# Two encoder layers on one Trainium2 core: the feed-forward's first norm applied as token factors behind the up projection

## The chip, the core and the metric

The kernel runs on one core of a Trainium2 chip. Its engines are TensorE (PE: matmuls; PEld: its weight loads), the vector engine (DVE), the scalar engine (ACT), GpSimd (POOL) and the engine that issues most loads (SP). Each works through its own list of instructions in order, and semaphores tie them together. SBUF has 128 partitions; matmul results land in PSUM, in banks of 128 x 512 float32. The metric is device time in microseconds (us) for one execution; 0.2% of it is 3 us.

## The reference, cut to what matters

Two layers act on x, 512 positions (tokens) of 1024 channels. Each has a token-mixing sub-layer and a feed-forward, and each of these has a norm before and a norm behind it. What the change touches is the end of the mixing sub-layer and the feed-forward:

```python
def rms_norm(x, g):
    y = xf * lax.rsqrt(jnp.mean(xf * xf, axis=-1, keepdims=True) + RMS_EPS)
    return y * g
...
    x = x + rms_norm(merged @ w_out[l], g_post_mix[l])
    h = rms_norm(x, g_pre_ffn[l])
    u = depthwise_conv_centred(h @ w_up[l], conv_w[l], conv_b[l])
    a, b = jnp.split(u, 2, axis=-1)
    f = jax.nn.gelu(a) * b
    x = x + rms_norm(f @ w_down[l], g_post_ffn[l])
```

`w_out` is 1024 x 1024, `w_up` 1024 x 5632, `w_down` 2816 x 1024. The convolution has width 3 and runs over positions, for each channel by itself. The factor rsqrt(...) is one number per token; the gain g is one number per channel.

## The kernel before, in words

**Layout.** Channels lie on partitions, tokens along the free axis. x is eight tiles of 128 channels x 512 tokens. A matrix of weights is cut into column tiles of 128 outputs; one tile of `w_up` or `w_out` is 128 x 8 x 128 (eight steps of 128 input channels, 512 KB).

**Split numbers.** Every operand of a large matmul is kept as two float32r numbers, a rounded high part and the rest. `split` (lines 220 to 222) makes them: a copy on ACT writes `hi`, a subtraction on DVE (or GpSimd) writes `lo`. One step of an output tile is three matmuls (`mm3`, line 246): high by high, high by low, low by high. A full tile has 8 steps of 512 columns (24 matmuls), a half tile 8 steps of 256.

**Weights.** `weights` (line 224) loads a tile into one of three buffers `wraw` and splits it, either into `whi` and `wlo` (two buffers each) or into buffers of another pool that are held longer (`m`, 32 buffers; `ka`, 12; `h`, 16).

**Order.** The program is written out by a Python generator in one order, and each engine executes its share of that order. `Woven` (line 46) keeps an estimate of TensorE's clock while matmuls are written. A job is a generator that yields a delay or a flag; `tick` runs the jobs that have come due between two steps of a tile, so their instructions land between the matmuls; `need` runs jobs until a flag is given. On TensorE this order is fixed by dependences; a matmul of a job stands where the job came due, and whatever is behind it waits with it.

**A norm.** `rstd_job` (line 323) sums squares over channels with matmuls against a column of 1/1024 (`mean`), takes the root on ACT and the reciprocal on DVE. That gives one factor per token, with tokens on partitions (`st`). To use it on tiles whose tokens lie on the free axis, it builds a diagonal matrix (two DVE multiplications of the identity, `h<-ident,st`) and multiplies it with a matrix of ones: the bank `pt` then has each token's factor in all 128 rows. The norms work on half the tokens (256) at a time; all 18 of the program go this way.

**The end of a mixing sub-layer** (`sublayer_end`, line 741, with `n_half` = 8). All eight tiles of `w_out` are done for half 0 (two at a time at first), then for half 1. ACT squares each result, DVE adds up the squares. When a half is complete, `end_job` (line 361) is spawned: norm, then per 128 channels a multiplication and the addition to x, and new squares in `acc2`; 9 us later `pre_norm_job` (line 347) makes the second norm from `acc2` and writes h = x * g * factor, split, for that half.

**The group.** Beside this stand six tiles of the up projection (0, 22, 1, 23, 2, 24; `run_group`, line 430), whose weights were split on GpSimd: half 0 of all six as soon as half 0 of h is there, then half 1. Two tiles go at a time. Their six banks are held until the convolution reads them.

**The loop** (line 860). For each of 22 pairs of up tiles j and j + 22: load and split weights, 24 matmuls into an `mm` bank (three banks), and `conv` (line 730): ACT writes y = bank * w1 + b, and two DVE operations of 511 columns add the neighbours, read from the bank. Gelu on ACT, the product and the split of the result on DVE. The weights of a tile are written directly before its matmuls. Then `sublayer_end` again, for `w_down` (three parts of weights per tile, 22 steps), with the last one or two tiles by halves, and in layer 0 the memory norm of layer 1 (`mem_norm_job`: squares on ACT, added up on GpSimd).

In the trace nearly all matmuls bear line 244 (`mm`), and nearly all ACT and DVE operations line 114, since helpers record them; the tile names tell them apart.

## Time and profile before

| | before |
|---|---|
| median of 3 runs (lowest, highest) | 1579.44 us (1579.17, 1579.61) |
| the profiled execution, its span | 1579.04 us, 1577.3 us |
| PE busy | 1529.7 us, 97% |
| PEld busy | 1316.4 us, 83% |
| DVE busy | 911.2 us, 58% |
| ACT busy | 727.4 us, 46% |
| GpSimd busy | 186.4 us, 12% |
| moved by DMA | 144.96 MB, 92 GB/s on average |
| mean granted clock of TensorE | 0.995 of full speed |

The span is the time from the first to the last instruction that the profile shows; the execution's own time is 1.7 us more. Busy time is the sum over an engine's instructions. 97% for PE means that about 48 us of the span hold no matmul; where they lie is not told by a share of the span, but by windows and by the column "idle before" of the timeline, which names the instruction that released the waiting one. The granted clock is the speed that the chip let TensorE have: 1.00 is 2.4 GHz, and the lower of its two levels is 1.2 GHz.

### The profile page before, as it was taken

The numbers are of one execution on the slowest core, as the hardware profiler recorded it, in microseconds if no ns is written. First come the engines' busy times: TensorE is split into PE (matmuls) and PEld (weight loads), VectorE is DVE, ScalarE is ACT, GpSimd is POOL, SyncE is SP. The second block draws the span as 40 slices with busy tenths as digits, with TensorE's granted clock in tenths as the row PEclk, the third lists the DMA queues.
The fourth block names the chain that finished last, engine by engine and source line by source line (L and its number), as shares of the span: only waits on it lengthen the run. The fifth ranks groups of instructions, "written<-read, shape, count | busy, mean of one in ns | idle before, by whom it ended". The sixth has DMA issues, their size and how long they took to land.

```text
span 1577.3 us, 21375 instructions
## 1 busy us (share of the span) xinstructions
PE 1529.7 (97%) x8246; PEld 1316.4 (83%) x8246; DVE 911.2 (58%) x1654; ACT 727.4 (46%) x1289; POOL 186.4 (12%) x244
## 2 busy tenths in 40 slices
PE   6999999999999999999989999999999999999997
PEld 5988888889898888878888888888898888888887
DVE  6686566344866666542386856743457666664233
ACT  5465575334544444532345646733454544444231
POOL 4340000110400000010062300001121000000000
PEclk9999999999999999999999999999999999999998
DMA  7222213224213222333331221132431232223331
GB/s 241 87 78 67 66 56 100 88 94 134 81 42 106 93 95 96 115 97 100 115 113 49 86 69 56 51 120 74 140 101 48 69 105 95 94 96 96 99 103 62
DMA packets 46614, 144.96 MB, mean 92 GB/s; under 512 B 5232, under 2 KB 11376, under 8 KB 46512
## 3 DMA queue, kind: packets, MB, share of 16 engines
q1 hardware_dynamic: 44656, 139.61, 27.7%
q10 hardware_dynamic: 1152, 2.10, 0.5%
q0 software_dynamic: 704, 1.88, 0.4%
q8 instruction: 65, 1.06, 0.3%
q14 instruction: 37, 0.30, 0.1%
HBM read 141.47 MB, written 2.10 MB: 91 GB/s over the span
## 4 chain that ended last, share of the span: by engine, by line
PE 88%; DVE 8%; ACT 2%; issue 1%; DMA 1%; SPq 0%; ACTq 0%
PE mm L244 73%; PE s L244 6%; PE o L244 3%; PE pt L244 2%; DVE h L114 2%; PE pt L255 2%; DVE y L114 2%; DVE x L114 1%; DVE m L114 1%; DVE wlo L114 1%; ACT whi L114 1%; DVE acc L114 1%; DVE ka L114 0%; ACT y L114 0%; DMA m<-in_memT_dram 0%
## 5 line engine op out<-in xcount | busy, mean ns | idle before, releaser
L244 PE MATMUL mm<-h,whi 128*128 128x512 f32 x2432 | 755.7, 392 | 0.0
L244 PEld LDWEIGHTS mm<-h,whi 128*128 128x128 f32 x2432 | 449.6, 188 | 88.7
L114 DVE TENSOR_TENSOR wlo<-wraw,whi 128x1024 fp32r<-128x1024 f32 (+1 forms) x203 | 246.9, 1218 | 394.9 <-ACT whi L114 394.8
L244 PE MATMUL mm<-h,wlo 128*128 128x512 f32 x1216 | 473.9, 390 | 0.0
L114 ACT CAST whi<-wraw 128x1024 fp32r<-128x1024 f32 (+1 forms) x203 | 210.3, 1038 | 296.5 <-PE mm L244 295.7
L244 PEld LDWEIGHTS mm<-h,wlo 128*128 128x128 f32 x1216 | 228.2, 188 | 48.5
L244 PE MATMUL mm<-m,whi 128*128 128x512 f32 (+1 forms) x672 | 178.2, 354 | 1.6 <-DVE m L114 0.8
L244 PEld LDWEIGHTS mm<-m,whi 128*128 128x128 f32 x672 | 119.6, 192 | 19.0 <-PE mm L244 1.3
L114 DVE SCALAR_TENSOR_TENSOR y<-mm,vec,y 128x511 f32<-128x511 f32 x160 | 118.9, 746 | 8.5 <-ACT y L114 5.9
L244 PE MATMUL mm<-m,wlo 128*128 128x512 f32 (+1 forms) x336 | 118.3, 352 | 0.7 <-DVE wlo L114 0.7
L114 ACT ACTIVATE y<-mm,vec 128x512 f32<-128x512 f32 (+1 forms) x163 | 113.6, 698 | 0.1
L244 PE MATMUL mm<-m,m 128*128 128x512 f32 (+1 forms) x432 | 88.6, 346 | 0.0
L222 POOL TENSOR_TENSOR m<-wraw,m 128x512 fp32r<-128x512 f32 x42 | 56.3, 1355 | 238.5 <-ACT m L114 234.2
L728 POOL TENSOR_TENSOR m<-m,y 128x512 f32<-128x512 f32 x28 | 36.1, 1289 | 405.7 <-DVE y L114 405.7
L244 PEld LDWEIGHTS mm<-m,m 128*128 128x128 f32 x432 | 67.6, 190 | 8.4
L244 PEld LDWEIGHTS mm<-m,wlo 128*128 128x128 f32 x336 | 64.4, 192 | 9.4 <-DVE wlo L114 1.1
L114 ACT ACTIVATE y<-y 128x512 f32<-128x512 f32 x44 | 27.8, 632 | 87.3 <-DVE y L114 87.3
L244 PE MATMUL mm<-h,m 128*128 128x256 f32 x456 | 63.6, 296 | 4.0 <-ACT h L114 1.6
L114 DVE TENSOR_TENSOR acc<-acc,sq 128x256 f32<-128x256 f32 (+1 forms) x86 | 44.6, 521 | 37.5 <-ACT sq L114 36.9
L114 ACT CAST m<-wraw 128x512 fp32r<-128x512 f32 (+1 forms) x98 | 56.1, 602 | 21.1 <-DMA wraw<-in_w_brb_dram 9.5
L244 PEld LDWEIGHTS mm<-h,m 128*128 128x128 f32 x456 | 59.2, 199 | 6.4 <-ACT h L114 2.8
L114 ACT CAST m<-pt 128x512 fp32r<-128x512 f32 (+1 forms) x72 | 38.2, 539 | 40.4 <-PE pt L255 32.0
(150 smaller groups left out, 1835.8 us busy)
## 6 DMA issues: line engine op xcount, KB each, us to landing
wraw<-in_w_in_dram SPq DMA_DIRECT2D x88, 512.0 KB, 3.3
wraw<-in_w_up_dram SPq DMA_DIRECT2D x88, 512.0 KB, 3.3
wraw<-in_w_down_dram SPq DMA_DIRECT2D x32, 512.0 KB, 3.5
wraw<-in_w_out_dram SPq DMA_DIRECT2D x16, 512.0 KB, 3.4
wraw<-in_w_down_dram SPq DMA_DIRECT2D x16, 384.0 KB, 3.1
wraw<-in_w_kv_dram SPq DMA_DIRECT2D x8, 512.0 KB, 3.6
wraw<-in_w_bra_dram SPq DMA_DIRECT2D x16, 192.0 KB, 2.3
x<-in_xT_dram SPq DMA_DIRECT2D x8, 256.0 KB, 7.2
```

Source lines behind the costliest of these rows:

```text
L114: return op(*args, **kw)
L222: last_lo[eng or V] = (eng or V).tensor_sub(lo, src, f32(hi)).ins
L244: wv.pe(nc.tensor.matmul(ps, a, b, start=first, stop=last), cost)
L255: wv.pe(nc.tensor.transpose(ps[:, 128 * i:128 * i + 128], s, ident), 0.11)
L728: (V if br == 2 and m >= 6 else G).tensor_add(acc[m], acc[m], gs)
```

## The change

**Broadcast.** `rstd_job` no longer builds a diagonal matrix. Per 128 tokens one matmul takes, as its weights, the column of factors read 128 times (stride 0) and multiplies it with the identity. The job yields 0.8 instead of 1.2 before it.

**End of the mixing sub-layer.** `n_half` goes from 8 to 4: `w_out` tiles 0 to 3 are full tiles, 4 to 7 half tiles. The group has four up tiles (0, 22, 1, 23) instead of six. Their weights are split on ACT and DVE, one tile after each of the four full tiles (`fill`). Four tiles go at a time in the group, with a flag per step of 128 channels.

**Factors.** In this place `factor_end_job` stands for `end_job` and `pre_norm_job`. It updates x as before, then splits x * g (without the factor of the second norm) as input of the up projection. The second norm's factors are worked out from the new x and copied to R, 128 x 512. Each up output is multiplied by R on DVE (`scaled`) on its way from the bank to SBUF, ahead of its convolution, which reads the SBUF tile. The product with the factor commutes with the matmul, since a factor belongs to a token.

**Weights and held outputs.** Up weights are loaded and split one tile ahead, and the first part of `w_down` ahead of the end of the loop. A pair of banks is held and read one tile later: the first waits for the flag of R, and up to j = 2 one held pair is processed per tile.

```diff
@@ rstd_job @@
         V.reciprocal(rs, rs)
-        diag = small("h32", 4, (128, n))
+        yield 0.8
         for b in range(nb):
-            V.tensor_scalar_mul(diag[:, 128 * b:128 * b + 128], ident, rs[:, b:b + 1])
-        yield 1.2
-        mm(pr, ones, diag, True, True, n * 4 / 2400.0)
+            one = rs[:, b:b + 1]
+            spread = bass.AP(one.tensor, one.offset, [list(one.ap[0]), [0, 128]])
+            mm(pr[:, 128 * b:128 * b + 128], spread, ident, True, True, 0.22)
+    def raw_split(l, goff, k, src, hi, lo):
+        g = vec[:, l, goff + k:goff + k + 1]
+        ACT.activation(hi, src, AF.Copy, scale=g)
+        V.scalar_tensor_tensor(out=lo, in0=src, scalar=g, in1=f32(hi), op0=ALU.mult, op1=ALU.subtract)
+    def scaled(ps, R):
+        y = ytile()
+        V.tensor_mul(y, ps, R)
+        return y
+    def factor_end_job(l, goff, og, acc, acc2, i, nxt):
+        half, box = HALVES[i], []
+        gnext, h, R = nxt
+        yield ready(1.4)
+        yield from rstd_job([acc[:, half]], 256, box)
+        for k in range(KD):
+            V.tensor_mul(og[k][:, half], og[k][:, half], box[0])
+            V.tensor_add(x[k][:, half], x[k][:, half], og[k][:, half])
+            raw_split(l, gnext, k, x[k][:, half], h[k][0][:, half], h[k][1][:, half])
+            if k == 0:
+                yield 0.6
+            wv.give(f"h{l}.{gnext}.{i}.{k}")
+            yield 1.05
+        for k in range(KD):
+            sumsq_add(acc2[:, half], x[k][:, half], k == 0)
+        yield 3.5
+        box = []
+        yield from rstd_job([acc2[:, half]], 256, box)
+        ACT.copy(R[:, half], box[0])
+        if i == 1:
+            yield 0.6
+            wv.give(f"R{l}.{gnext}")
@@ run_group @@
-        for i in range(0, len(ws), 2):
+        for i in range(0, len(ws), side):
             for k in range(n):
+                if flag and side > 2:
+                    wv.need(f"{flag}.{k}")
@@ conv @@
-        y = ytile()
+        u, y = scaled(ps, R), ytile()
@@ sublayer_end @@
             one(m, mmbank(), w_of(m, None), FULL, m == 0)
+            if m < len(fill):
+                fill[m]()
@@ the layer @@
-        up = (0, 22, 1, 23, 2, 24)
-                     ms, 8, lambda a, i, l=l, hs=hs: pre_norm_job(l, V_PREF, a, hs, i))
-        gw = group_weights([w_up[l, m] for m in up], (G,) * 6)
+        up = (0, 22, 1, 23)
+                     ms, 4, (V_PREF, hs, R), fill=[lambda m=m: gw.extend(group_weights([w_up[l, m]], (V,))) for m in up])
+        rest = [m for j in range(NFF) for m in (j, j + NFF) if m not in pss]
+        ahead = [weights(w_up[l, rest[0]], KD, 128)]
         for i in range(2):
-            run_group((gw, pss), hs, HALVES[i], f"h{l}.{V_PREF}.{i}")
+            run_group((gw, list(pss.values())), hs, HALVES[i], f"h{l}.{V_PREF}.{i}", None, 4)
+                w = ahead.pop()
+                rest.pop(0)
+                if rest:
+                    ahead.append(weights(w_up[l, rest[0]], KD, 128))
+                pair.append(mmbank())
+                linear(pair[-1], w, hs)
+                if held:
+                    wv.need(flag)
+                    mixed(*held.pop(0))
+            held.append((j, pair))
+            if not rest:
+                ahead.append(weights(w_down[l, 0, :, 0:8, :], 8, 128))
+            if j > 2 or j == NFF - 1:
+                while held:
+                    mixed(*held.pop(0))
```

How this moves instructions is shown at three places. The first is TensorE at the first step of the up group of layer 0, half 0; h are the split inputs (high and low in turn), m the split weights. Before:

```order
L244 MATMUL mm_4324<-h_3614,m_4266 128x256
L244 MATMUL mm_4324<-h_3615,m_4266 128x256
L244 MATMUL mm_4324<-h_3614,m_4267 128x256
L244 MATMUL mm_4325<-h_3614,m_4276 128x256
L244 MATMUL mm_4325<-h_3615,m_4276 128x256
L244 MATMUL mm_4325<-h_3614,m_4277 128x256
L244 MATMUL mm_4324<-h_3616,m_4266 128x256
L244 MATMUL mm_4324<-h_3617,m_4266 128x256
L244 MATMUL mm_4324<-h_3616,m_4267 128x256
```

The same place now:

```order
L242 MATMUL s_4113<-h_3606,m_3670 128x256
L242 MATMUL s_4113<-h_3607,m_3670 128x256
L242 MATMUL s_4113<-h_3606,m_3671 128x256
L242 MATMUL s_4114<-h_3606,m_3715 128x256
L242 MATMUL s_4114<-h_3607,m_3715 128x256
L242 MATMUL s_4114<-h_3606,m_3716 128x256
L242 MATMUL o_4115<-h_3606,m_3760 128x256
L242 MATMUL o_4115<-h_3607,m_3760 128x256
L242 MATMUL o_4115<-h_3606,m_3761 128x256
L242 MATMUL mm_4116<-h_3606,m_3805 128x256
L242 MATMUL mm_4116<-h_3607,m_3805 128x256
L242 MATMUL mm_4116<-h_3606,m_3806 128x256
```

Before, the second pair of inputs (h_3616, h_3617) is asked for after six matmuls; now after twelve, four tiles to a step.

The second place is the vector engine in the same layer, at half 0's norms (acc sums squares, y are the outputs of `w_out`, x the residual, pt the broadcast factors). Before, from the reciprocal of the second norm on:

```order
L114 RECIPROCAL st_4131<-st_4131 128x2
L114 TENSOR_SCALAR h_869_4134<-ident,st_4131 128x128 x2
L114 TENSOR_TENSOR acc_3640<-acc_3640,sq_870_4140 128x256
L114 SCALAR_TENSOR_TENSOR h_872_4155<-x_85,vec,pt_4128 128x256
L114 SCALAR_TENSOR_TENSOR h_873_4159<-x_85,vec,pt_4128 128x256
L114 SCALAR_TENSOR_TENSOR h_874_4163<-x_85,vec,pt_4128 128x256
L114 TENSOR_TENSOR h_3615<-h_872_4155,h_3614 128x256
```

Now, from the reciprocal of the first norm on:

```order
L114 RECIPROCAL st_3987<-st_3987 128x2
L114 TENSOR_TENSOR y_3625<-y_3625,pt_3984 128x256
L114 TENSOR_TENSOR acc_3633<-acc_3633,sq_864_3996 128x256
L114 TENSOR_TENSOR x_85<-x_85,y_3625 128x256
L114 TENSOR_TENSOR y_3626<-y_3626,pt_3984 128x256
L114 TENSOR_TENSOR y_3627<-y_3627,pt_3984 128x256
L114 SCALAR_TENSOR_TENSOR h_3607<-x_85,vec,h_3606 128x256
```

The input of the up projection (h_3615 before, h_3607 now) was made behind the second norm's reciprocal, diagonal matrix and broadcast; now it follows the first norm's broadcast, a product and a sum.

The third place is the scalar engine where layer 0's down projection begins (h and sq are squares of the memory norm, ka the split of the last Gelu product, whi the high part of `w_down`). Before:

```order
L114 ACTIVATE y_6184<-mm_6159,vec 128x512
L384 DMA h_6222<-in_memT_dram 128x512
L114 ACTIVATE h_1201_6224<-h_6216 128x256
L114 ACTIVATE sq_1202_6226<-h_6216 128x256
L114 ACTIVATE sq_1203_6229<-h_6218 128x256
L114 ACTIVATE sq_1204_6232<-h_6218 128x256
L114 ACTIVATE sq_1205_6235<-h_6220 128x256
L114 ACTIVATE sq_1206_6238<-h_6220 128x256
L114 CAST ka_6190<-y_6149 128x512
L114 ACTIVATE sq_1207_6241<-h_6222 128x256
L114 ACTIVATE sq_1208_6244<-h_6222 128x256
L114 CAST whi_6270<-wraw_6268 128x1024
```

Now:

```order
L114 ACTIVATE y_6051<-y_6049,vec 128x512
L114 ACTIVATE h_1206_6085<-h_6077 128x256
L114 ACTIVATE sq_1207_6087<-h_6077 128x256
L114 ACTIVATE sq_1208_6090<-h_6079 128x256
L114 ACTIVATE sq_1209_6093<-h_6079 128x256
L114 ACTIVATE sq_1210_6096<-h_6081 128x256
L114 ACTIVATE sq_1211_6099<-h_6081 128x256
L114 ACTIVATE sq_1212_6102<-h_6083 128x256
L114 ACTIVATE sq_1213_6105<-h_6083 128x256
L114 CAST ka_6057<-y_6045 128x512
L114 CAST whi_6131<-wraw_6129 128x1024
```

The cast of the last product stood before the last two squares and now stands behind them; the first cast of `w_down` that follows was that of its first part, and is now that of its second.

## Rows read from the trace of the kernel before

**Rows 1.** The table of stretches. Columns: the stretch (us from the span's start), its length, the busy us of PE, PEld, DVE, ACT and POOL with the number of instructions, the granted clock as a part of full speed, the DMA engines' share, GB/s.

```profile
369.70:458.60 88.90, 84.37 (x693) 83.24 (x693) 61.08 (x130) 45.34 (x103) 16.16 (x12) 1.00 0.24 78
458.60:665.30 206.70, 206.70 (x914) 171.13 (x913) 126.93 (x154) 90.63 (x116) 0.00 (x0) 1.00 0.29 96
784.00:860.00 76.00, 68.96 (x521) 65.80 (x521) 58.60 (x127) 36.43 (x83) 36.25 (x61) 1.00 0.27 89
1145.40:1236.40 91.00, 87.13 (x693) 85.78 (x692) 60.98 (x130) 45.36 (x103) 16.12 (x12) 0.96 0.24 76
1180.00:1190.00 10.00, 6.79 (x43) 6.17 (x42) 7.74 (x16) 4.98 (x14) 3.52 (x3) 0.81 0.22 70
375.00:385.00 10.00, 10.00 (x86) 10.00 (x85) 4.16 (x9) 4.68 (x12) 0.00 (x0) 1.00 0.65 211
```

**Rows 2.** TensorE's timeline at the end of the mixing sub-layer, in layer 0 and (the last two rows) in layer 1. Columns: start in us, duration in us, engine, line, operation, output and inputs, shape, number of instructions in the row, and in brackets the idle time before it and its releaser. `pt<-mean,acc` sums the squares over channels, `pt<-h,ones` is the broadcast of the factors.

```profile
369.05 0.51 PE L244 MATMUL mm<-m,ka 128*128 128x256 f32 x3
...
380.39 3.04 PE L244 MATMUL mm<-m,m 128*128 128x256 f32 x24
383.27 3.04 PE L244 MATMUL s<-m,m 128*128 128x256 f32 x24
...
409.29 0.58 PE L244 MATMUL pt<-mean,acc 128*128 128x1 f32 x4 [2.32 <-DVE acc L114]
...
437.11 0.50 PE L244 MATMUL pt<-mean,acc 128*128 128x1 f32 x4
437.47 0.60 PE L244 MATMUL o<-h,m 128*128 128x256 f32 x3
...
438.98 0.60 PE L244 MATMUL pt<-h,ones 128*128 128x256 f32 x2
439.23 0.70 PE L244 MATMUL o<-h,m 128*128 128x256 f32 x3
439.77 0.52 PE L244 MATMUL pt<-h,m 128*128 128x256 f32 x3
...
458.55 0.63 PE L244 MATMUL mm<-h,whi 128*128 128x512 f32 x2
...
1144.70 0.52 PE L244 MATMUL mm<-m,ka 128*128 128x256 f32 x3
...
1236.36 0.63 PE L244 MATMUL mm<-h,whi 128*128 128x512 f32 x2
```

**Rows 3.** The chain of work that ended last, cut to 372 to 475 us: three full up tiles behind each other (start, duration, engine, tile, line, number of matmuls).

```profile
458.71 16.35 PE mm L244 x72
```

**Rows 4.** The vector engine's timeline in the same piece: products with the broadcast factors and the second norm's multiplications (columns as in rows 2).

```profile
426.51 0.75 DVE L114 TENSOR_TENSOR y<-y,pt 128x256 f32<-128x256 f32 x2 [0.85 <-PE pt L244]
...
439.62 1.26 DVE L114 SCALAR_TENSOR_TENSOR h<-x,vec,pt 128x256 f32<-128x256 f32 x3 [0.99 <-PE pt L244]
```

**Rows 5.** The timeline at the end of layer 0's down projection: the two diagonal matrices of its norms on DVE, and the broadcasts on TensorE that waited for them.

```profile
785.34 2.12 DVE L114 TENSOR_SCALAR h<-ident,st 128x128 f32<-128x128 f32 x2
787.61 0.67 PE L244 MATMUL pt<-h,ones 128*128 128x256 f32 x2 [1.27 <-DVE h L114]
...
810.15 2.35 DVE L114 TENSOR_SCALAR h<-ident,st 128x128 f32<-128x128 f32 x2
812.65 0.67 PE L244 MATMUL pt<-h,ones 128*128 128x256 f32 x2 [3.04 <-DVE h L114]
```

**Rows 6.** The other broadcasts for which TensorE waited, in its timeline: two near the start, one at layer 1's memory norm, one at the very end.

```profile
12.90 1.19 PE L244 MATMUL pt<-h,ones 128*128 128x256 f32 x2 [1.16 <-DVE h L114]
...
47.13 0.67 PE L244 MATMUL pt<-h,ones 128*128 128x256 f32 x2 [0.25 <-DVE h L114]
...
685.34 0.67 PE L244 MATMUL pt<-h,ones 128*128 128x256 f32 x2 [0.43 <-DVE h L114]
...
1568.34 0.99 PE L244 MATMUL pt<-h,ones 128*128 128x256 f32 x2 [1.16 <-DVE h L114]
```

**Rows 7.** Groups by line, operation, tile and shape over the whole span: number, busy us, mean ns of one, and the idle time before them with its releaser.

```profile
L114 DVE TENSOR_TENSOR wlo<-wraw,whi 128x1024 fp32r<-128x1024 f32 x190 | 234.0, 1233 | 359.6 <-ACT whi L114 359.4
L114 ACT CAST whi<-wraw 128x1024 fp32r<-128x1024 f32 x190 | 199.5, 1052 | 262.6 <-PE mm L244 261.8 <-DVE m L114 0.4
L114 DVE SCALAR_TENSOR_TENSOR y<-mm,vec,y 128x511 f32<-128x511 f32 x160 | 118.9, 746 | 8.5 <-ACT y L114 5.9
L114 DVE TENSOR_TENSOR y<-y,y 128x512 f32<-128x512 f32 x44 | 31.0, 704 | 4.4 <-ACT y L114 2.8
L114 DVE TENSOR_TENSOR y<-mm,y 128x512 f32<-128x512 f32 x32 | 21.9, 684 | 0.0
```

**Rows 8.** The DMA issues of the page: the loads of `w_out`, number, KB each, median us from issue to landing.

```profile
wraw<-in_w_out_dram SPq DMA_DIRECT2D x16, 512.0 KB, 3.4
```

**Rows 9.** The timeline of all engines where layer 0's down projection begins (columns as in rows 2).

```profile
667.17 7.73 POOL L318 TENSOR_TENSOR h<-h,sq 128x256 f32<-128x256 f32 x7 [241.79 <-ACT sq L114]
668.09 1.19 DVE L114 TENSOR_TENSOR y<-y,y 128x512 f32<-128x512 f32 x1
...
670.47 1.76 ACT L114 CAST whi<-wraw 128x1024 fp32r<-128x1024 f32 x2
671.55 0.73 PE L244 MATMUL mm<-m,whi 128*128 128x512 f32 x2 [0.65 <-ACT whi L114]
...
672.96 0.50 PE L244 MATMUL mm<-m,wlo 128*128 128x512 f32 x1 [0.68 <-DVE wlo L114]
```

60 lines of the change are left out of this document (29 added, 31 removed).

## The prediction

> **What bounds the kernel now.** I read the table of stretches first, because a share over the whole span hides where TensorE waits. In the up projection's loop it never waits: 206.70 us busy of 206.70, with the vector engine at 126.93 and GpSimd at nothing [rows 1]. In three other stretches it does: the end of the mixing sub-layer of each layer (84.37 of 88.90 us and 87.13 of 91.00) and the end of layer 0's down projection (68.96 of 76.00). So a change is worth what it takes out of these waits, plus what it takes out of TensorE's own work, and extra vector work in the loop costs nothing until it fills 206.7 us.
>
> Next I read TensorE's timeline at the first of these ends, for starts and waits [rows 2]. Output tiles of `w_out` begin at 369.05 and the first full up tile at 458.55: 89.50 us. In layer 1 the same piece runs from 1144.70 to 1236.36: 91.66 us. A half tile (24 matmuls of 256 columns) starts 2.88 us after the one before (380.39 and 383.27). A full tile (24 of 512) takes 16.35 / 3 = 5.45 us [rows 3], 0.31 us less than its two halves. The longest wait is at 409.29: the sum of squares of half 1 is not yet there. Behind it come sqrt, reciprocal, the diagonal matrix, a broadcast, the residual, a second sum of squares with a second broadcast, and the multiplication; only then may the up projection start. That is two norms in a row, with too little matmul work beside them. Layer 1 pays 2.16 us more for the same work, and there the granted clock is 0.81 of full speed in the ten microseconds around the pause (1180 to 1190), so part of it ran at 1.2 GHz [rows 1].
>
> **The change, part by part.** *Work of the two ends.* Before, the piece has 28 half tiles (16 of `w_out`, 12 of the six up tiles). Now `w_out` has 4 full and 8 half tiles, the group 8 half tiles, and two of the old six become full tiles. That is 6 x 5.45 + 16 x 2.88 = 78.8 us against 28 x 2.88 = 80.6. Into it go four norms, each a pair of sums (437.11 to 437.47, 0.36) and a broadcast (438.98; the next tile's three matmuls, normally 0.36, are followed by its successor only 0.79 after it, so some 0.43) [rows 2]: 3.2 us. Without waits the piece is 82.0 us; I take 82.3.
>
> *Is it without waits?* The factor of the second norm leaves the path: the up projection now reads x times the gain. Per 128 rows the vector engine does a multiplication (0.75 / 2), an addition that I take to last as long, and one scalar-tensor-tensor (1.26 / 3) [rows 4]: 1.2 us, with the square sums some 1.5. Eight need 9.6 to 12 us. Half 0's norm is asked for 2.2 us after its last tile, and 9.4 us of half tiles plus 1.44 us per step of the new group of four lie beside it, so the first step is asked for at about 11.5 us and the last at 21.6; the first is ready at some 6.5, the last at 16. For half 1 the group's first half (11.5 us) is the cover. No wait is left in either. The factors R themselves are only needed when the first held tile is read, behind the whole group.
>
> So I count 89.5 - 82.3 = 7.2 us in layer 0 and 91.7 - 82.3 = 9.4 in layer 1 (no pause, so no clock drop): **16.6 us**. From below: if only the shapes come and all waits stay, 2 x 1.8 = 3.6 us.
>
> *The broadcast without its diagonal matrix.* It goes in all 18 norms, but pays only where TensorE sat waiting for it. In the end of layer 0's down projection the two multiplications that build it took 2.12 and 2.35 us, and TensorE waited 1.27 and 3.04 us [rows 5]; with it gone the broadcast follows the reciprocal, and the second wait also shrinks by the earlier start. I take 4.0 of 7.04 us idle there; bounds 2.0 and 5.5. At the start (1.16 and 0.25 waited) I take 0.7, at layer 1's memory norm 0.4 (0.43 waited), at the very end 0.5 of 1.16, where the chain stands alone [rows 6]. Sum **5.6**. The new broadcast, two 128-column matmuls that read one column of weights 128 times, stands in no row. The old one, of as many columns, lets the next tile start 0.25 us later (438.98 to 439.23) and lasts 0.67 alone [rows 2, 6]: from no difference to two of 0.67, so 0 to +0.67 us each. I take +0.1, the nearer row being the one in a running stream; it is in the 82.3 above.
>
> *The added multiplication.* 44 tiles per layer get one vector operation more, 0.684 us (nearest row: a product read from the same kind of accumulator bank) [rows 7]. Per pair of tiles the vector engine then has 2 x 0.684 + 2 x 1.233 + 4 x 0.746 + 2 x 0.704 (the product after Gelu and its subtraction) = 8.2 us, against 2 x 5.45 = 10.9 of TensorE. It is hidden, and each bank is read once and free 0.7 us after its tile. The convolution's reads move from the bank to SBUF; the trace shows no such form at 511 columns, but the SBUF-only form of 512 in the same group lasts 0.704, so I keep the price. If the cover were gone the loop would stretch by the excess over 10.9.
> The Trainium skill speaks against the part: its page "VectorE: DVE Perf Modes", section "Rules for kernel authors", says not to fuse but to keep the number of operations down, because each one drains the pipeline. By that rule the 88 operations cost an estimated 60 us of the vector engine; by the stretches row they fall into its 80 us of idle time per layer and cost the kernel nothing.
>
> *The way into the loop.* The factors come about 2.6 us after the group's last matmul. Four held banks are then read; the fourth must be free when the third full tile starts, some 11.7 us after the group. On the vector engine there lie before it four scaling products, six convolution steps, one weight split and one product: 2.7 + 4.5 + 1.2 + 0.7 = 9.1 us, from 2.6: 11.7. It comes out even. With the wait for the Gelu table I put 0.3 us per layer, 0 to 3.
>
> *Weights.* Four up tiles are split among the first four `w_out` tiles; the third of these needs its load and split by 10.9 us. Its buffer comes free at about 4.2, the load takes 3.4 [rows 8], the split 1.05 + 1.23 [rows 7]: 9.9. It fits by 1 us.
>
> *Into the down projection.* The first part of `w_down` is now ready early, but in layer 0 the second part's cast stands behind all seven squares of the memory norm, which GpSimd's additions pace at 7.73 / 7 = 1.1 us each; before, it ended its 1.76 us pair at 672.2 behind them, and TensorE waited 0.65 and 0.68 us [rows 9]. The convolution's result starts 0.7 us later and the cast moves behind the last two squares too: **-1.0 us** (0 to -2).
> A rule of the Trainium skill would add to this: "SBUF — State Buffer", section "Who interferes with whom", has a vector operation with two SBUF inputs and a GpSimd one exclude each other. The scaled convolution now has two SBUF inputs, right beside those additions. By the rule an estimated 1 us more is lost in layer 0; the sum here goes without it.
>
> **Sum.** 16.6 + 5.6 - 0.6 - 1.0 = 20.6 us. The profiled execution took 1579.04 (span 1577.3 and 1.7 around it): 1558.4. The median of the runs lies 0.4 above it: **1558.8 us**.
>
> **Rivals.**
> *The wait moves to the factors.* The chain into the loop comes out even, so a late table load or square sum makes TensorE wait for a bank. For it: four banks are held and the vector engine has no slack for 12 us. Against: it catches up 2.7 us per pair afterwards. Price: one tile, 5.45 us per layer, gives 1558.8 + 10.9 = 1569.7 us.
> *Weights too late: slower.* Through three raw buffers 14 loads must pass in `w_out`'s 44.8 us, 3.2 us each, so a buffer may turn round in 9.6 us. It eats the gain if the turn exceeds (44.8 + 10.3) / 14 x 3 = 11.8. Three loads at once at the 211 GB/s of the row at 375 us take 7.4 [rows 1]; with 2.3 for the split and 3 of waiting behind evictions in the scalar engine's order it is 12.7, that is 59.3 us, 14.5 more per layer: 1588 us. Against: a single load lands in 3.4, and only ten of the fourteen fall inside the piece.
> *The vector engine becomes the bound* (what the skill's rule on the number of operations fears). It needs operations 33% longer than their rows, 10.9 / 8.2. At the 1.7 times that a product takes beside GpSimd elsewhere (1.19 against 0.704) [rows 7, 9] it would be 3 us per pair, over 1650 us in all. Against: GpSimd is idle in the loop.
>
> **Chances.** My forecast 0.66, on its own 1553 to 1565 (the bounds of the broadcast, of the way in and of the down projection's end). The wait at the factors 0.18. Weights late 0.08, vector engine 0.03. Gains and new waits that cancel 0.05. A range of 1552 to 1573 takes in the first two. Within 0.2% (3 us, about what a measurement of this kernel can tell from no change): 0.05; slower 0.11; faster 0.84.
>
> **What would show it.** In the profile after: no wait of TensorE between the start of `w_out` and the first full up tile, that piece at 82 to 83 us in both layers, and a granted clock of 1.00 throughout layer 1's. The loop at 5.45 us per tile with the vector engine near 75%. A wait for a scaling product at the third full tile speaks for the first rival, one for `whi` or `wlo` in `w_out` for the second, tiles longer than 5.45 for the third. TensorE's wait at layer 0's second down part should be near 2.3 us. I am wrong if the piece stays above 86 us, or if the end of layer 0's down projection keeps its 7 us of idle time.

## The result, and the profile after

The changed kernel takes 1563.16 us (median of 4 runs, 1562.61 to 1565.10) where the kernel before, timed beside it, takes 1579.31: a ratio of 0.9902, 95% interval 0.9885 to 0.9919. I had forecast 1558.8, in a range of 1552 to 1573. So 16.1 us came of the 20.6 that I had added up. The profiled execution is the slowest of the four (1565.10, span 1563.3), and its working is told against the profiled one of before (span 1577.3): 14.0 us. Of all executions told of here one, the fourth of experiment 6, was in a slow state (1700.84 us at a mean granted clock of 0.849) and is left out.

TensorE's starts in the two timelines cut both spans into the same stretches:

| stretch | before, us | after, us | difference | forecast |
|---|---|---|---|---|
| start to layer 0's `w_out` | 369.05 | 367.32 | -1.73 | -0.7 |
| layer 0, `w_out` to the down projection | 296.25 | 288.52 | -7.73 | -6.9 |
| down projection to its first square sums | 119.00 | 121.72 | +2.72 | +0.6 |
| from there to layer 1's first full tile | 62.87 | 66.23 | +3.36 | -4.0 |
| on to layer 1's `w_out` | 297.53 | 297.51 | -0.02 | 0 |
| layer 1, `w_out` to the down projection | 298.40 | 288.72 | -9.68 | -9.1 |
| down projection to the end | 134.20 | 133.28 | -0.92 | -0.5 |

Half of the first row is not the change's: TensorE's first matmul starts at 9.90 us before and at 9.04 after, and at 8.71 to 9.97 in the kernels of the experiments.

The table of stretches of the changed kernel (columns as in [rows 1]): end of the mixing sub-layer in layer 0, its loop, the way into the down projection, the end of the down projection with a part of it, and the end of the mixing sub-layer in layer 1.

```profile
367.30:437.66 70.36, 70.36 (x510) 66.60 (x508) 45.83 (x99) 38.70 (x83) 0.00 (x0) 1.00 0.31 98
439.49:655.84 216.35, 216.35 (x957) 179.20 (x956) 163.91 (x210) 102.77 (x128) 0.00 (x0) 1.00 0.30 96
660.00:675.00 15.00, 11.98 (x45) 9.08 (x44) 6.19 (x5) 4.08 (x6) 5.34 (x6) 0.89 0.22 63
775.41:843.79 68.38, 61.58 (x488) 61.09 (x487) 49.45 (x106) 32.77 (x76) 33.23 (x56) 0.93 0.28 89
805.00:820.00 15.00, 9.63 (x68) 9.45 (x67) 11.96 (x23) 5.15 (x12) 7.43 (x8) 0.77 0.45 148
1141.30:1211.83 70.53, 70.53 (x509) 66.80 (x508) 45.85 (x99) 38.67 (x83) 0.00 (x0) 1.00 0.30 98
```

The first, second and last rows answer to those of [rows 1] for the same places: TensorE has no idle time left at either end (70.36 of 70.36, 70.53 of 70.53), the clock is 1.00 there, and the loop is full with the vector engine at 163.91 / 216.35 = 76%. The fourth row is the end of layer 0's down projection, which 784.00:860.00 showed before with other bounds: 6.8 us are idle there, of 7.04, and the clock is now 0.93, with 0.77 in its worst part (the fifth row).

TensorE's timeline at those places (columns as in [rows 2]):

```profile
437.29 0.50 PE L242 MATMUL pt<-mean,acc 128*128 128x1 f32 x4
437.66 0.71 PE L242 MATMUL mm<-h,whi 128*128 128x512 f32 x2
...
663.26 0.74 PE L242 MATMUL mm<-m,whi 128*128 128x512 f32 x2 [1.81 <-ACT whi L114]
...
665.20 0.50 PE L242 MATMUL mm<-m,wlo 128*128 128x512 f32 x1 [1.20 <-DVE wlo L114]
...
791.52 0.58 PE L242 MATMUL pt<-mean,acc 128*128 128x1 f32 x4 [1.43 <-DVE acc L114]
...
802.59 0.38 PE L253 MATMUL s<-ident,m 128*128 128x128 f32 x2
802.88 0.71 PE L242 MATMUL pt<-ident,st 128*128 128x128 f32 x4
...
807.01 0.52 PE L242 MATMUL s<-h,m 128*128 128x256 f32 x3
812.91 7.13 PE L242 MATMUL s<-h,m 128*128 128x256 f32 x45 [5.37 <-DVE m L114]
```

The group's last sums come at 437.29 and the first full tile at 437.66, with nothing between. The waits of [rows 5] for the two broadcasts are gone (`pt<-ident,st` has no bracket), but two others, which are the whole of the 6.8 us, stand in their place. The first half's second norm waits 1.43 us for its square sums (791.52). And 4 us after the second broadcast TensorE waits 5.37 us: the group's fourth tile needs an `s` bank, in which the second memory value was transposed at 802.59. In the kernel before, the matmuls at these two places waited 0 and 0.83 us, and the second half's square sums behind them (825.00) did not wait:

```profile
799.44 0.50 PE L244 MATMUL pt<-mean,acc 128*128 128x1 f32 x4
...
817.38 5.63 PE L244 MATMUL s<-h,m 128*128 128x256 f32 x45 [0.83 <-DVE m L114]
...
825.00 0.50 PE L244 MATMUL pt<-mean,acc 128*128 128x1 f32 x4
```

What empties the bank now is on the vector engine (and, before that, a cast on the scalar engine at 810.61):

```profile
803.63 0.75 DVE L114 TENSOR_TENSOR y<-y,pt 128x256 f32<-128x256 f32 x2 [0.16 <-PE pt L242]
804.30 2.12 DVE L114 TENSOR_TENSOR x<-x,y 128x256 f32<-128x256 f32 x2
...
807.88 1.48 DVE L114 TENSOR_TENSOR acc<-acc,sq 128x256 f32<-128x256 f32 x1
...
810.61 1.82 DVE L114 TENSOR_TENSOR x<-x,y 128x256 f32<-128x256 f32 x2
812.35 0.41 DVE L114 TENSOR_TENSOR m<-s,m 128x256 fp32r<-128x256 f32 x1
```

The products and sums of x for the second half follow the broadcast directly now, and the bank's `m<-s` stands behind them. Three rows are 2.4 to 3.6 times as long as their like (a pair of sums 0.75, a single one 0.41 elsewhere).

### The profile page after: what moved, and what is told of

Same layout as the page of the kernel before. It is cut to its first block, busy times and chain, and to the rows that moved or that the text cites. A ratio compares the mean times of both kernels' runs of the same rounds, so it can differ in the third digit from the quotient of the medians.

```text
span 1563.3 us, 20698 instructions
## 1 busy us (share of the span) xinstructions
PE 1524.4 (98%) x7994; PEld 1303.7 (83%) x7994; DVE 945.2 (60%) x1682; ACT 735.1 (47%) x1267; POOL 155.2 (10%) x219
## 4 chain that ended last, share of the span: by engine, by line
PE 54%; DVE 3%; issue 0%; ACT 0%; ACTq 0%; DVEq 0%
PE mm L242 48%; PE s L242 3%; PE o L242 2%; PE pt L242 1%; PE pt L253 1%; DVE y L114 1%; DVE x L114 1%; DVE m L114 0%; DVE acc L114 0%; DVE wlo L114 0%; DVE ka L114 0%; DVE st L114 0%; ACT sq L114 0%; ACT y L114 0%; ACT m L114 0%
## 5 line engine op out<-in xcount | busy, mean ns | idle before, releaser
L242 PE MATMUL mm<-m,whi 128*128 128x512 f32 (+1 forms) x800 | 216.3, 358 | 2.7 <-ACT whi L114 1.8
L242 PEld LDWEIGHTS mm<-m,whi 128*128 128x128 f32 x800 | 142.5, 190 | 25.1 <-ACT whi L114 2.2
L242 PE MATMUL mm<-m,wlo 128*128 128x512 f32 (+1 forms) x400 | 142.8, 357 | 1.2 <-DVE wlo L114 1.2
L114 DVE SCALAR_TENSOR_TENSOR y<-y,vec,y 128x511 f32<-128x511 f32 x176 | 130.9, 750 | 3.5 <-ACT y L114 0.9
L114 DVE TENSOR_TENSOR y<-mm,R 128x512 f32<-128x512 f32 x82 | 56.4, 688 | 68.5 <-PE mm L242 68.5
L114 ACT ACTIVATE y<-y,vec 128x512 f32<-128x512 f32 x88 | 71.0, 813 | 2.2 <-DVE y L114 1.9
L242 PE MATMUL mm<-m,m 128*128 128x512 f32 x240 | 63.6, 395 | 0.0
L242 PE MATMUL s<-h,m 128*128 128x256 f32 x384 | 54.7, 290 | 5.4 <-DVE m L114 5.4
L114 ACT ACTIVATE y<-mm,vec 128x512 f32<-128x512 f32 (+1 forms) x91 | 57.4, 631 | 0.1
L114 DVE TENSOR_TENSOR m<-pt,m 128x512 fp32r<-128x512 f32 (+1 forms) x72 | 45.0, 629 | 18.3 <-ACT m L114 17.4
```

The source lines that it names most:

```text
L114: return op(*args, **kw)
L242: wv.pe(nc.tensor.matmul(ps, a, b, start=first, stop=last), cost)
```

## The experiments

Times are medians; the ratio is to the kernel before, run on the same chip. From chip to chip the median of the kernel before went from 1578.27 to 1579.81 us, so a difference of some 1.5 us or less between two experiments is not told apart. Three dots stand for lines left out.

**1. The broadcast alone**, in the kernel before.

```diff
-        diag = small("h32", 4, (128, n))
+        yield 0.8
         for b in range(nb):
-            V.tensor_scalar_mul(diag[:, 128 * b:128 * b + 128], ident, rs[:, b:b + 1])
-        yield 1.2
-        mm(pr, ones, diag, True, True, n * 4 / 2400.0)
+            one = rs[:, b:b + 1]
+            spread = bass.AP(one.tensor, one.offset, [list(one.ap[0]), [0, 128]])
+            mm(pr[:, 128 * b:128 * b + 128], spread, ident, True, True, 0.22)
```

> The kernel before with one part of the change, the broadcast without the diagonal matrix. In the changed kernel the end of layer 0's down projection (from the half tile whose matmuls number 18 before the first sums, 782.16 us before and 775.41 after, to the first full tile of layer 1) takes 68.4 us where it took 65.0; I had forecast 4.0 us less. Theory A: the broadcast itself is the cause. With the diagonal gone the second half's products and sums of x move ahead of the split of the second memory value, which empties the bank that the next group's second tile needs. Then this kernel shows the same wait of some 5 us for that split and the same 68 us; the small gains elsewhere (start 0.9, memory norm 0.6, very end 0.9, ends of the mixing sub-layers about 2) give 1579.3 - 4.4 + 3.4 = 1578. Theory B: another part of the change (weights ahead, shapes) disturbs that place, and the broadcast brings what I forecast: 1579.3 - 5.6 - 2.0 = 1572, with the stretch at 61.

1577.45 us, ratio 0.9987 (0.9978 to 0.9996). Theory A: the same wait, in the same place of TensorE's timeline, and from the first square sums to layer 1's first full tile 64.50 us (62.87 before).

```profile
817.56 6.94 PE L242 MATMUL s<-h,m 128*128 128x256 f32 x45 [5.25 <-DVE m L114]
```

So the loss at this end belongs to the broadcast, and the broadcast as a whole brings about 2 us (0.6 to 3.5 by the interval). The tile that waits is the second of its pair, as the expectation has it, and the fourth of the group.

**2. The second memory value first.**

```diff
+            up = V.tensor_mul(og[k][:, half], og[k][:, half], box[0]).ins
+            if then is not None and i and k == 0:
+                behind(up, memv[0])
...
+        memv[0] = last_lo[V]
```

> The changed kernel; at the end of layer 0's down projection the first product with the second half's broadcast factors may only be issued on the vector engine behind the split of the second memory value. Theory A (order of issue): TensorE's wait of 5.37 us at the second tile of the group goes and with it the stretch at 0.77 of the clock behind it, so the stretch of 68.4 us shrinks to about 62 and the run takes 1563.2 - 6 = 1557. Theory B (the split comes late because vector operations beside GpSimd's subtractions last two to three times as long, 2.12 us for two sums of x): the order matters little, the split is still slowed, and the gain stays under 2 us: 1561 to 1563.

1562.40 us, 0.9889 (0.9874 to 0.9903): B by the number, by neither theory's mechanism, and not told apart from the changed kernel (0.9902). The wait for the value fell to 1.20 us, and the next one uncovered, for the sums that the second half's second norm needs:

```profile
806.21 5.66 PE L243 MATMUL s<-h,m 128*128 128x256 f32 x45 [1.20 <-DVE m L114]
...
816.21 0.58 PE L243 MATMUL pt<-mean,acc 128*128 128x1 f32 x4 [2.90 <-DVE acc L114]
```

**3. The squares of the memory norm later.**

```diff
         acc = small("h32", 3)
+        if l:
+            yield 7.0
         for k in range(KD):
```

> The changed kernel with the squares of layer 1's memory norm written 7 us later, behind the cast of the second part of w_down. Theory A (the cast stands behind squares that GpSimd's additions pace): TensorE's waits of 1.81 and 1.20 us at that part go, and with them the low clock behind them (22 matmuls in 6.88 us instead of 5.28). That is up to 4.6 us: 1563.2 - 4.6 = 1558.6, or 1560 if the unprofiled runs did not have the low clock. Theory B (the convolution's late result is what holds the scalar engine): the cast is no earlier than its split, the wait moves to the split and less than 1 us is gained: 1562.5.

1559.89 us, 0.9872 (0.9857 to 0.9886): 3.3 us less, theory A. Both waits at the second part of `w_down` are gone: the first two parts run from 655.43 to 666.31, where the third starts, 10.88 us for two times eight steps. GpSimd's additions still run beside the vector engine there (a product takes 1.23 us at 659.80), so moving the cast ahead of the squares is enough.

**4. Without the exchange of factors.** The second norm stands ahead of the up projection again; shapes, broadcast and weights ahead stay.

```diff
-        u, y = scaled(ps, R), ytile()
+        u, y = ps, ytile()
...
-                     ms, 4, (V_PREF, hs, R), fill=[lambda m=m: gw.extend(group_weights([w_up[l, m]], (V,))) for m in up])
+                     ms, 4, lambda a, i, l=l, hs=hs: pre_norm_job(l, V_PREF, a, hs, i), fill=[lambda m=m: gw.extend(group_weights([w_up[l, m]], (V,))) for m in up])
...
-            run_group((gw, list(pss.values())), hs, HALVES[i], f"h{l}.{V_PREF}.{i}", None, 4)
+            wv.need(f"h{l}.{V_PREF}.{i}")
+            run_group((gw, list(pss.values())), hs, HALVES[i], None, None, 4)
...
-                    wv.need(flag)
```

> The changed kernel without the exchange of factors: the second norm is applied ahead of the up projection as in the kernel before, the convolution reads the bank; shapes of the end, broadcast, weights ahead and one held pair per tile stay. Theory A (the exchange takes two waits out of each end): the waits come back, the piece from the start of w_out to the end of the loop grows by about 7.7 - 1.8 = 6 us in layer 0 and 9.7 - 1.8 = 8 in layer 1: 1563.2 + 14 = 1577. Theory B (fuller tiles and the earlier broadcast had already closed them): within 2 us of 1563.

1578.89 us, 0.9992 (0.9982 to 1.0001). Theory A, and a little more than it: the two stretches from `w_out` to the down projection take 297.81 and 297.23 us, as long as before (296.25 and 298.40). The fuller tiles gain nothing by themselves; the two norms in a row wait in other places, and the clock falls (0.96 from 367 to 447).

```profile
413.93 0.58 PE L242 MATMUL pt<-mean,acc 128*128 128x1 f32 x4 [1.50 <-DVE acc L114]
415.47 0.91 PE L242 MATMUL pt<-mean,acc 128*128 128x1 f32 x4 [0.97 <-DVE acc L114]
...
435.09 0.38 PE L242 MATMUL s<-h,m 128*128 128x256 f32 x1 [1.01 <-ACT h L114]
```

**5. Three orders together**: experiments 2 and 3, and `yield 10.5` instead of 9.0 ahead of the second half's second norm in layer 0's down projection.

> The changed kernel with three changes of order: the two that ran before (the second memory value's split ahead of the second half's products; squares of the memory norm behind the cast of the second part of w_down), and the second half's second norm in layer 0's down projection due 10.5 us instead of 9.0 behind the sums of x. With the split ahead alone TensorE still waited 2.90 us for the square sums of that norm and 1.20 for the split. Theory A (the order decides, and each wait removed uncovers the next until the vector engine's own work ends last): the late squares give 3.3 as measured alone, the order of the split 0.8 as measured alone, and the later due time half of 2.90 and of the low clock behind it, some 2: 1563.2 - 6 = 1557. Theory B (the vector engine's chain is the bound, wherever TensorE's part is written): the two known gains only, 1559.

1558.09 us, 0.9862 (0.9846 to 0.9879). Between the theories: the wait of 2.90 fell to 1.68, 1.27 stayed at the value, and the stretch takes 64.50 us. Beside experiment 3 the intervals overlap.

**6. Every scaling product twice.**

```diff
         V.tensor_mul(y, ps, R)
+        V.tensor_mul(y, ps, R)
```

> The changed kernel with every scaling product done twice: 88 more vector operations of 0.688 us, 60.5 us of the vector engine. Theory A (its idle time hides them, but the way into the loop is even): in the loop tiles stay at 5.44 us, with the vector engine at (163.9 + 27.5) / 216.4 = 88% there; only the third full tile waits, for the fourth held bank, which came free 0.26 us before it (448.64 against 448.90) and now comes 4 x 0.688 - 0.26 = 2.5 us late: 1563.2 + 5 = 1568. Theory B (each operation costs more than its row, by its start and end): the loop stretches, by 10 us or more in all: above 1573.

1568.20 us, 0.9929 (0.9913 to 0.9946). Theory A, at the place named. (The third full tile starts at 449.12 in the changed kernel, not at 448.90 as I wrote, so the fourth bank is free 0.48 us ahead of it.)

```profile
450.51 0.69 DVE L114 TENSOR_TENSOR y<-mm,R 128x512 f32<-128x512 f32 x1
...
451.34 0.70 PE L242 MATMUL mm<-h,whi 128*128 128x512 f32 x2 [2.47 <-ACT y L114]
...
1224.56 0.71 PE L242 MATMUL mm<-h,whi 128*128 128x512 f32 x1 [2.48 <-ACT y L114]
```

The bracket names ACT, but the last read of that bank is the second product, which ends at 450.51 + 0.69 = 451.20. Behind it no wait stands until the down projection at 658.18. The stretch from `w_out` to there is 2.8 us longer than in the changed kernel, in layer 1 it is 4.4, since there the clock fell behind the same wait (shown at the end). The vector engine has room in the loop, and almost none at its entrance.

**7. The memory norm's additions on the vector engine**: `MSQ = V`.

> The changed kernel with the additions of layer 1's memory norm on the vector engine instead of GpSimd (seven of 128 x 256, 0.42 us each). Theory A (vector operations slow down beside GpSimd): with GpSimd idle the convolution's pair, 1.94 us there, falls to the 1.54 that it takes in the loop, the product from 1.11 to 0.70, the weight splits from 3.17 to 2.47 a pair; the squares are paced at 0.4 instead of 1.1 us, and of the waits of 1.81 and 1.20 us at most 1 is left: 1563.2 - 3 = 1560. Theory B (they are long there for another reason): the durations stay, the vector engine has 2.9 us more in front of the splits, and the wait stays at 3 or grows: 1563 to 1566.

1559.32 us, 0.9872 (0.9857 to 0.9887). Theory A, by the time and by the durations. The vector engine's timeline at that place in the changed kernel, with GpSimd's row, and then in this one, where GpSimd is idle:

```profile
658.28 7.45 POOL L316 TENSOR_TENSOR h<-h,sq 128x256 f32<-128x256 f32 x7 [301.60 <-ACT sq L114]
...
657.62 1.94 DVE L114 SCALAR_TENSOR_TENSOR y<-y,vec,y 128x511 f32<-128x511 f32 x2 [0.89 <-ACT y L114]
659.60 1.11 DVE L114 TENSOR_TENSOR y<-y,y 128x512 f32<-128x512 f32 x1
...
663.38 3.17 DVE L114 TENSOR_TENSOR wlo<-wraw,whi 128x1024 fp32r<-128x1024 f32 x2
```

```profile
658.79 0.75 DVE L114 SCALAR_TENSOR_TENSOR y<-y,vec,y 128x511 f32<-128x511 f32 x1
...
659.79 0.69 DVE L114 TENSOR_TENSOR y<-y,y 128x512 f32<-128x512 f32 x1
...
660.73 1.22 DVE L114 TENSOR_TENSOR wlo<-wraw,whi 128x1024 fp32r<-128x1024 f32 x1
```

Seven additions more on the vector engine, and yet it is done earlier; both waits of 1.81 and 1.20 are gone. The run does not part two effects of taking GpSimd away: the vector operations are short, and the squares no longer wait for GpSimd's additions, so that the cast of the second part runs at 659.51, ahead of the last product's cast and the last two squares (at 662.17 in the changed kernel, behind them).

**8. Without weights ahead.**

```diff
-        ahead = [weights(w_up[l, rest[0]], KD, 128)]
+        ahead = []
...
-                w = ahead.pop()
-                rest.pop(0)
-                if rest:
-                    ahead.append(weights(w_up[l, rest[0]], KD, 128))
+                w = weights(w_up[l, rest.pop(0)], KD, 128)
...
-            if not rest:
-                ahead.append(weights(w_down[l, 0, :, 0:8, :], 8, 128))
```

> The changed kernel without weights ahead: each up tile's weights are written directly before its matmuls, as in the kernel before, and the first part of w_down too; the rest stays. Theory A (the scheduler already splits a tile's weights as soon as their buffer is free, so writing them earlier moves little but the first part of w_down): the loop stays at 216.4 us, at most a wait of 1 to 2 us at its beginning, and the wait at the second part of w_down goes from 3.0 to the 1.3 of the kernel before: 1561 to 1565. Theory B (with the scaling products in the vector engine's order the splits come late without it): a wait at each of the first tiles or more, 1570 and above.

1568.01 us, 0.9926 (0.9911 to 0.9940): between the theories. Each layer has one wait, 0.95 us for a weight split at the fourth full tile (456.65 and 1230.40), and its stretch from `w_out` is 1.2 us longer. The waits at the second part of `w_down` stayed at 1.82 and 1.20, against my expectation: they do not come from writing weights ahead. (Experiment 4, which writes ahead but has no exchange of factors, waits 0.65 and 0.68 us there, as the kernel before.) Of the 4.8 us between the medians 2.5 lie in these stretches; where the rest lies its profile, an execution 1.6 us under its median, does not show.

**9 and 10. Another order of banks** in layer 1's first group, alone and with experiment 7.

```diff
+        if l:
+            return [mmbank(), mmbank(), obank(128), tbank(), sbank(), sbank()]
```

> The changed kernel; in layer 1 the first group takes its banks in another order, so that its third and fourth tiles use the o and pt banks and the two s banks, in which the memory values were transposed, are asked for 5.8 us later. Nothing on the vector or scalar engine is put in another order by hand. Theory A (TensorE's 5.37 us were a wait for one bank, while the sums that come next are ready in time because x was updated first): the wait goes and no other takes its place, nor the low clock behind it: the stretch from layer 0's down projection's start to layer 1's first full tile shrinks from 187.95 to about 181, and 1563.2 - 6.5 = 1556.7. Theory B (as when the split was put first: the next wait, for the second half's square sums, uncovers): 1 to 3 us, 1560 to 1562.

> The same order of banks, and the memory norm's additions on the vector engine. The two places lie 140 us apart, so the gains should add: 1563.2 - 3.9 (measured alone) - 6.5 = 1552.8 by theory A of the banks, 1557 to 1559 by its theory B.

1565.19 us, 0.9904 (0.9888 to 0.9921), and 1558.41 us, 0.9862 (0.9845 to 0.9878). Experiment 9 is as fast as the changed kernel: theory A falls, and B's 1 to 3 us do not come either. Experiment 10 ends where B put it, 0.9 us under experiment 7, with overlapping intervals. The wait for the bank is gone from both, and in its place TensorE waits for the second half's square sums:

```profile
818.65 0.98 PE L242 MATMUL pt<-mean,acc 128*128 128x1 f32 x4 [3.56 <-DVE acc L114]
```

That is experiment 9; in 10 it is 3.03 us. There the vector engine's long rows can be set against GpSimd's:

```profile
797.45 2.05 DVE L114 TENSOR_TENSOR x<-x,y 128x256 f32<-128x256 f32 x2
...
800.96 1.52 DVE L114 TENSOR_TENSOR acc<-acc,sq 128x256 f32<-128x256 f32 x1
...
803.73 1.86 DVE L114 TENSOR_TENSOR x<-x,y 128x256 f32<-128x256 f32 x2
...
796.49 2.73 POOL L220 TENSOR_TENSOR m<-wraw,m 128x512 fp32r<-128x512 f32 x2 [3.58 <-PE s L253]
800.62 1.57 POOL L220 TENSOR_TENSOR m<-wraw,m 128x512 fp32r<-128x512 f32 x1 [1.41 <-ACT m L114]
803.91 1.39 POOL L220 TENSOR_TENSOR m<-wraw,m 128x512 fp32r<-128x512 f32 x1 [1.72 <-ACT m L114]
```

Each long row ends 0.28 to 0.29 us behind the end of a row of GpSimd (799.50 and 799.22, 802.48 and 802.19, 805.59 and 805.30).

**11. The broadcast and the banks**, in the kernel before.

> The kernel before with the broadcast alone, and the same order of banks in layer 1's first group. With the bank out of the way the broadcast should bring at the end of layer 0's down projection what I had forecast for it: 4.0 us of its 7.04 us of waits, against a loss of 1.6 with the broadcast alone (64.50 against 62.87). Theory A: the stretch from the first square sums to layer 1's first full tile takes 59 us and the run 1577.5 - 5.6 = 1572. Theory B (the gain was never there, since the vector engine's chain through two norms ends last): 62 to 63 us, 1575 to 1576.

1575.74 us, 0.9969 (0.9955 to 0.9983): the median of theory B, though the stretch is 65.38 us and not 62 to 63; again a wait for the sums takes over (3.10 us at 823.07). (The profiled execution is the slowest, 2.0 us above the median.) The gain of 4.0 us is not there with the bank out of the way either.

**12. The group's subtractions on the vector engine**: `GEN = 'GGVVVV'`, on top of experiment 10.

> The kernel with the order of banks and the memory norm's additions on the vector engine, and now also the four subtractions of layer 1's group weights that GpSimd did beside the second half's sums of x (128 x 512, 796 to 805 us) on the vector engine. There a pair of sums of x took 2.05 and 1.86 us instead of 0.75, and a square sum 1.52 instead of 0.41: 3.5 us more. Theory A (a vector operation that reads two tiles of SBUF stands still while GpSimd's subtraction runs): these rows fall to 0.75 and 0.41, the vector engine has four subtractions of 0.66 more, 2.6 us, so from the second half's first square sums to its second 15.1 us instead of 16.05, the wait of 3.03 us there about 2.1 and the run 1558.4 - 1 = 1557.4. Theory B (they are long for another reason, or the subtractions go in front of the sums): the rows stay long or the distance grows to 18 us: 1560 or more.

1556.99 us, 0.9861 (0.9845 to 0.9878), the lowest of all, though not told apart from experiments 5 and 10. The number is theory A's, the way is not. The rows became short, as theory A has it, but not the distance: the second half's square sums come at 794.91 and 811.13, 16.2 us apart (16.05 before), and the wait stays at 3.14.

```profile
798.48 0.41 DVE L114 TENSOR_TENSOR x<-x,y 128x256 f32<-128x256 f32 x1
...
801.70 0.42 DVE L114 TENSOR_TENSOR acc<-acc,sq 128x256 f32<-128x256 f32 x1
...
809.18 1.80 DVE L114 TENSOR_TENSOR acc<-acc,sq 128x256 f32<-128x256 f32 x2
...
808.13 2.58 POOL L565 TENSOR_TENSOR y<-mask,y 128x256 f32<-128x256 f32 x3 [2.53 <-DVE acc L114]
```

The four subtractions and a row beside GpSimd's next work, the biases of the attention, took the time saved.

## Why the prediction was right, and where it was not

**The two ends.** The 16.6 us were 17.4, less nothing for the way into the loop. With the forecast's own tiles (38 of 5.44 us) taken off, the piece is 81.8 us in layer 0 and 82.0 in layer 1, against 82.0 without waits in the working and the 82.3 that I took. Experiment 4 shows what carries it: without the factors the ends are as long as before. My lower bound (the shapes alone give 3.6 us) was thus no bound; they give nothing while the norms are in a row. The factors with the old shapes were not tried.

**The added multiplication** is hidden, as by the stretches row: 0.688 us each, the loop at 76%. The Trainium skill's rule on the number of operations ("VectorE: DVE Perf Modes", section "Rules for kernel authors") did not bear here: experiment 6 puts another 60 us of operations on the vector engine for a wait of 2.5 us per layer, all of it at the entrance. That the way in "comes out even" was right to half a microsecond: the first rival lay one doubled product away.

**The weights** were in time: no wait in `w_out`.

**The broadcast** is the step that failed. I took 4.0 of 7.04 us at the end of layer 0's down projection because TensorE's brackets there named the diagonal matrix [rows 5], and I did not ask what TensorE needs next and when that is ready. Both waits went, and 3.4 us were lost: TensorE's idle time from the first square sums to layer 1's first full tile went from 5.94 to 6.80 us, and its busy time from 56.93 to 59.43, with the clock at 0.92 there instead of 1.00 (columns as in [rows 1], before and after):

```profile
784.30:847.17 62.87, 56.93 (x462) 55.80 (x461) 51.81 (x113) 30.27 (x72) 33.30 (x56) 1.00 0.30 97
777.56:843.79 66.23, 59.43 (x470) 58.94 (x469) 48.43 (x105) 30.89 (x72) 33.23 (x56) 0.92 0.29 92
```

(Kernels with the same code at this place, experiments 1, 3, 4 and 6 to 8, lost 1.6 to 3.2.) By the sign that I had set (the 7 us of idle time stay) this part of the forecast was wrong. Two things are shown. The loss comes with the broadcast (experiment 1): the vector engine went on to the sums of x before it emptied the bank, and behind the pause the clock fell, so that 45 matmuls took 7.13 us where they take 5.63 to 5.66 at full clock (experiment 2: 5.66). And the gain was not to be had by freeing the bank: in experiments 2, 5 and 9 to 12 TensorE waits next for the second half's square sums, which come 16.0 to 17.6 us behind the half's first ones, at the end of a chain of products, sums of x and squares on the vector engine. The kernel before left 17.6 us between the two (807.36 to 825.00) and did not wait there, so this part had at most 1.6 us to give. The first half shows the same: the broadcast's wait of 1.27 us went, and one of 1.43 us for the square sums came. The whole stretch stayed at 62.4 to 66.2 us in all kernels (62.87 before). The second half's first sums themselves come 11 us behind the end of its last tile in the changed kernel (801.43 and 790.09), 9 before; whether an earlier place would now pay was not tried. In the other places the broadcast gave about what I had put, or more: 0.55 us at the start (experiment 1, `w_out` at 368.50) for 0.7, 0.6 at the memory norm for 0.4, 0.9 at the end for 0.5; and in a running stream it takes 0.36 us of TensorE (404.01 to 404.37), the 0.25 of the old one and the 0.1 that I had added.

**Into the down projection** the mechanism was right and the size was not: 1.0 forecast, 3.3 found (the 2.72 of the table and the 0.6 that the memory norm gave back). Of these 1.7 are waiting: 3.0 us, where I had named 2.3 and the kernel before waited 1.33. The other 1.6 are a low clock behind the waits (0.89 in the third row of the stretches), for which the sum had no term; experiment 2, with the same two waits and the clock at 1.00 behind them, is 1.6 us shorter here. What holds the cast is what I had named, the squares that GpSimd's additions pace. The scalar engine's timeline in the changed kernel:

```profile
660.19 0.42 ACT L114 ACTIVATE sq<-h 128x256 f32<-128x256 f32 x1 [0.72 <-POOL h L316]
661.34 0.42 ACT L114 ACTIVATE sq<-h 128x256 f32<-128x256 f32 x1 [0.72 <-POOL h L316]
...
662.17 1.77 ACT L114 CAST whi<-wraw 128x1024 fp32r<-128x1024 f32 x2
```

These two casts are of the second and third parts of `w_down`, and so are the two behind the squares in the kernel before (670.47). In both kernels the cast of the first part starts with the last up tile, ahead of the squares (659.83 before, 650.38 now): it was ready early before, too, and what I said of the third place of the change, that the first part's cast stood behind the squares there, is wrong.

The sum also left the interference with GpSimd out. The Trainium skill's page "SBUF — State Buffer", section "Who interferes with whom", which I had set beside it, says that a vector operation with two SBUF inputs and a GpSimd operation that reads SBUF exclude each other. The trace agrees: with GpSimd idle beside them a product of 1.11 us falls to 0.69 (experiment 7), and a square sum of 1.52 to 0.42 (10 and 12). By the rows it is at most a part of what made the loss larger than forecast: the last product and its subtraction were as long in the kernel before (1.19 us at 668.09, 1.27 at 669.97); the convolution's pair grew by 0.4 (1.54 us at 666.52, 1.94 now) and the two weight splits by 0.4 (2.78 at 671.53, 3.17 now); and in experiment 3 both waits are gone with GpSimd at work. Its share was not measured by itself.

**The sum.** In the profiled execution the broadcast at the end of layer 0 came out 7.4 us worse than forecast and the way into the down projection 2.3; the two ends came out 1.4 better, the start 1.0 (0.9 of it the earlier first matmul), the memory norm and the very end 0.6. The bounds that I had set for the broadcast there, 2.0 and 5.5 us of gain, did not hold it. That the time still lies in the range is owed to the two ends, whose mechanism was right, and to the width of the range.

## What to carry to other kernels

When a wait is to be removed, read the next thing that its engine needs and when that is ready; where an engine off the path works through one long chain, each wait removed only uncovers the next, and the gain must be read from the chain's end. Taking a factor out of a chain of two norms carried the gain here: without it, and with the rest of the change left in, 15.7 of 16.1 us are gone (experiment 4). Fuller tiles were worth nothing without it; with it they make 3.6 us of the gain by the working, which no run shows by itself. An engine that is free by its share can still be late at the first tiles of a loop, and a helper engine can cost more than it does.

## What the hardware showed that was not expected

The same pause did not always cost the same. Experiments 2 and 9 both wait 1.8 us and then 1.2 or 0.9 us at the second part of `w_down`; these are the rows of eleven microseconds that begin ahead of the second wait, first of 2, then of 9:

```profile
664.00:675.00 11.00, 9.80 (x43) 7.70 (x43) 4.26 (x3) 1.55 (x3) 2.14 (x2) 1.00 0.37 100
```

```profile
664.00:675.00 11.00, 10.14 (x34) 7.89 (x34) 3.73 (x3) 1.05 (x1) 1.61 (x2) 0.72 0.29 86
```

At 1.00 of the clock 43 matmuls fit, at 0.72 only 34: nine matmuls of 0.23 us (9.80 / 43), some 2.1 us. The changed kernel lay between (0.89 from 660 to 675). Behind the wait of 1.43 us for the first half's square sums the clock was 0.83 in the changed kernel (791.52 to 801.43), and 1.00 behind the same wait in experiment 1 (797.71 to 808.00). Experiment 6 shows it within one execution: at the entrance of the loop TensorE waits 2.47 us in layer 0 and 2.48 in layer 1, and these are the eleven microseconds behind it in each:

```profile
451.34:462.34 11.00, 11.00 (x48) 9.09 (x49) 11.00 (x17) 4.48 (x7) 0.00 (x0) 1.00 0.28 96
1224.56:1235.56 11.00, 11.00 (x41) 8.92 (x42) 9.99 (x15) 4.32 (x6) 0.00 (x0) 0.84 0.19 62
```

The price of a pause here is thus its length plus 0 to about 2 us, and one profiled execution does not tell which.
